# A hybrid recurrent and attention trunk on one core: sums of the readout moved from GpSimd to VectorE, one-input steps moved to ScalarE, and one masked copy of the gated recurrence made a plain copy

## The chip, the cores and the metric

The kernel runs on one core of one Trainium2 chip. The metric is device time in microseconds (us), the median of three runs. A core has five engines that the profile names PE (TensorE matmul; PEld is its weight load), DVE (VectorE), ACT (ScalarE), POOL (GpSimd) and SP (SyncE, which only issues DMAs here). Each engine works through its own queue in order.

## What is computed

Two layers of a trunk over 2048 latent tokens and 256 context tokens, 1024 channels, all in float32. Each layer normalises, projects the channels once, and splits the result into three groups: an RWKV-7 recurrence (6 heads), a gated recurrence (HGRN2, 4 heads) and a windowed attention (6 heads). A readout joins them. Cut to what the change touches:

```python
# gated recurrence, per chunk (b = cumulative sum of log forget gates)
att = jnp.sum(q_c[..., :, None, :] * k_c[..., None, :, :] * jnp.exp(diff), axis=-1)   # lower triangle
out = o_inter + jnp.einsum('zbhts,zbhsv->zbhtv', att, v_c)

# readout of the RWKV heads
yc = y - jnp.mean(y, axis=-1, keepdims=True)
yn = yc * lax.rsqrt(jnp.mean(yc * yc, axis=-1, keepdims=True) + GN_EPS)
yn = yn.reshape(B, T, RWKV_W) * gn_w + gn_b
bonus = jnp.sum(_heads(r) * _heads(k) * r_k, axis=-1, keepdims=True) * _heads(v)
ya = (yn + bonus) * jax.nn.silu(g)
# readout of the gated recurrence
yb = (o * lax.rsqrt(jnp.mean(o * o, axis=-1, keepdims=True) + NORM_EPS)).reshape(...) * norm_w * jax.nn.silu(g)

y = jnp.concatenate([ya, yb, yt], axis=-1) @ w_out[l]
x = x + gate * y
```

## The kernel before

Each layer has three stages. The **input projection** makes all features and writes them to DRAM. The **recurrence stage** (`phase2`) runs four streams side by side: 36 RWKV steps, two directions of the gated recurrence (`Hgrn.window`, nine windows of 256 tokens each), and the attention. The **readout stage** (`Readout`) follows for nine windows of 256 tokens in layer 0 and eight in layer 1, where the context's window is not needed.

The order on each engine is set by a scheduler that replays the program against its own model of durations; `phase2` only hands it the streams in an interleaved order, the readout's at a lower priority. The queues are then fixed: an instruction that waits on the chip holds all that stand behind it on its engine.

`Hgrn.window` builds the attention matrix of a 128-token chunk in levels: a diagonal, then block sizes 1 to 64 (`products`, L1075 to L1085). For each level POOL subtracts (tile `hE`), ACT takes the exponential, DVE multiplies (`hE`, `hQz`), PE multiplies matrices into the PSUM tile `wps` (two buffers, shared with the attention), and the result is copied into `hatt`. At block size 64 the copy is a plain one on ACT. At all others two copies of 64 partitions are made by DVE under a mask (`copy_predicated`, L1085): 14 of them for a window and a direction, of which the block size 32 has two.

`Readout.__init__` splits the output weights, in eight pieces, into a rounded part on ACT (`wohi`) and the remainder on POOL (`wolo`, L1403); this falls into the end of the recurrence stage. `outputs(w)` prepares a window: it adds the two directions (L1455 on DVE, L1456 on POOL), and takes means by matmuls with a constant block matrix. For that `blocks` (L1424) splits its operand into a rounded copy `obh` (a DVE cast, L1430) and a remainder `obl` (DVE), and lets PE multiply both into `ops`. It is called seven times for a window, four times with 512 columns and three with 256. The scales `rk`, `gnw` and the bias `gnb` ride on fused DVE instructions of 256 columns (L83, a helper: `or` is r times k, `oY` the normalised output). At its end ACT rounds the whole result to `ohi`, and the remainder `olo` is made on POOL for the attention's 768 columns and on DVE for the other 1280. `project(w)` then runs 96 matmuls of 512 columns for a window, 24 into each PSUM tile `opo`; DVE multiplies a finished one by the gate (`og`), and POOL adds it to the residual `ox` (L1512). Program order puts `project(w)` beside `outputs` of the next window.

Helper lines: L64 is ACT's activation, L67 a matmul, L74 a two-input operation on DVE or POOL, L83 the fused DVE operation.

Of the kernel before, what the change touches and what calls it, by code (L numbers as in the profile page):

```python
# [9 lines left out]
F32 = mybir.dt.float32  # L10
# [9 lines left out]
L = 2  # L20
# [966 lines left out]
class Hgrn:  # L987
# [23 lines left out]
    def window(self, z, s):  # L1011
# [62 lines left out]

        def products(lhs, rhs, lv, out):  # L1075
            ps = P_([128, 4, 2, 32])
            for u in range(4):
                for e in range(2):
                    t.mm(ps[half[e], u], lhs[:, u, half[e]], rhs(u, e))
            for e in range(2):  # L1080
                o = out(half[e], slice(64 * e, 64 * e + 64))
                m, d = self.lm[half[e], z:z + 1, lv].to_broadcast([64, 8, 32]), ps[half[e]].rearrange("p u x t -> p (u x) t")
                if len(o.shape) == 4:
                    m, d = (a.rearrange("p u (m h) -> p u m h", h=o.shape[3]) for a in (m, d))
                nc.vector.copy_predicated(o, m, d)  # L1085
# [12 lines left out]
        for lv, h in enumerate((64, 32, 16, 8, 4, 2)):  # L1098
# [18 lines left out]
            else:  # L1117
                products(u4(E), lambda u, e: Qz[:, :, u, 32 * e:32 * e + 32], lv - 1, lambda r, c: qh(att[r, :, c]))
            yield
# [268 lines left out]
class Readout:  # L1388


    def __init__(self, t, l, ph):
# [7 lines left out]
        for k in range(KD):  # L1399
            w = ow.tile([128, D], F32, name="wo", tag="wo")  # L1400
            nc.sync.dma_start(out=w, in_=io["w_out"][l, :, k])
            t.act(self.whi[:, k], w, AF.Identity)
            t.tt(self.wlo[:, k], w, self.whi[:, k].bitcast(F32), ALU.subtract, nc.gpsimd)  # L1403
        self.bones = st.tile([128, 128], F32R, name="bonesr")
# [16 lines left out]
    def outputs(self, w):  # L1421
# [3 lines left out]
        def blocks(m, a, n):  # L1425
# [3 lines left out]
            e = cut(self.T_([128, 2, 256], "obl", CFG["bl"], F32R)[:, 0:n])  # L1429
            nc.vector.tensor_copy(h, a)  # L1430
            t.tt(e, a, h.bitcast(F32), ALU.subtract)
# [17 lines left out]
        t.tt(y0, y0, y1, ALU.add, nc.gpsimd if CFG["b2"] else None)  # L1449
        t.tt(Y[:, 3:5], h0, h1, ALU.add, nc.gpsimd)  # L1450
        yv = y0.rearrange("p c (i t) -> p i c t", i=3)
        for i0, n in ((0, 2), (2, 1)):
            ps = blocks(self.cen, yv[:, i0:i0 + n], n)
            t.act(SQ[:, i0:i0 + n], ps[:, 0:n], AF.Square)
            t.act(Y[:, i0:i0 + n], ps[:, 0:n], AF.Identity)  # L1455
        t.act(SQ[:, 3:5], Y[:, 3:5], AF.Square)  # L1456
        for i in range(3):
            t.stt(r[:, i], r[:, i], W(t.P(l, "rk"), i), k[:, i], ALU.mult, ALU.mult)
        yield
# [7 lines left out]
        for i0, n in ((0, 2), (2, 1)):  # L1467
            ps = blocks(self.bones, r[:, i0:i0 + n], n)
            t.tt(v[:, i0:i0 + n], v[:, i0:i0 + n], ps[:, 0:n], ALU.mult)
        hs = load(it(S["sgh"]), "or", [128, 2, 256])  # L1470
        yield
        for i in range(5):
            t.stt(Y[:, i], Y[:, i], W(t.P(l, "gnw"), i) if i < 3 else W(t.P(l, "hnw"), i - 3), SQ[:, i], ALU.mult, ALU.mult)
            if i < 3:
                t.stt(Y[:, i], Y[:, i], W(t.P(l, "gnb"), i), v[:, i], ALU.add, ALU.add)
        t.tt(Y[:, 0:3], Y[:, 0:3], sg, ALU.mult)
# [3 lines left out]
        for a, b, y in ((5, 8, yav), (0, 5, nt(Y))):  # L1480
            t.act(nt(hi[:, a:b]), y, AF.Identity)
            t.tt(nt(lo[:, a:b]), y, nt(hi[:, a:b]).bitcast(F32), ALU.subtract, nc.gpsimd if a == 5 or CFG["b3"] else None)
        self.y[w] = hi, lo
        yield

    def project(self, w, src, dst):
# [8 lines left out]
        for m in range(2):  # L1495
# [3 lines left out]
            for e in range(2):  # L1499
# [10 lines left out]
                else:  # L1510
                    t.tt(o, ps, g[:, d], ALU.mult)
                t.tt(x[:, d], x[:, d], o, ALU.add, nc.gpsimd if l < L - CFG["xa"] else None)  # L1512
                yield
# [137 lines left out]
```

## Time and profile before

| what | value |
|---|---|
| median of 3 runs | 4400.89 us (4397.25 to 4402.82) |
| the profiled execution: its own time, its span | 4410.3 us, 4408.5 us |
| mean granted clock of TensorE | 0.940 |
| PE busy | 3907.5 us (89%), 39424 matmuls |
| DVE busy | 2993.5 us (68%) |
| ACT busy | 2173.6 us (49%) |
| POOL busy | 893.3 us (20%) |

The busy times are sums over the whole span; a busy PE is not a PE at its peak, since matmuls overlap. In time the span is: input projection of layer 0 to about 1120 us, its recurrence stage to about 2000 us, its readout to 2262 us, then the same three for layer 1 to about 3350 us, 4165 us and the end.

### The profile page before, as it was taken

What the parts mean: (1) busy time and instruction counts of PE and PEld (TensorE: products, weight loads), DVE (VectorE), ACT (ScalarE), POOL (GpSimd) and SP (SyncE); (2) the same over time, 40 slices, a digit from 0 to 9 for tenths busy, and PEclk for the clock granted to TensorE, in tenths of its full rate; (3) what the DMA queues carried; (4) which work ended last, traced back from release to release, by engine and by line L of the source; (5) the groups of instructions that cost most, each with busy time, mean ns of one, the idle gap of its engine ahead of it and who ended that gap; (6) DMA issues with size and microseconds to landing.
All of it is one profiled execution on the core that took longest, in us unless ns stands there. A gap on an engine that the chain in (4) does not pass through costs nothing. (4 is left out here: it accounts for less than half of the span.)

```text
span 4408.5 us, 98655 instructions
## 1 busy us (share of the span) xinstructions
PE 3907.5 (89%) x39424; PEld 3188.1 (72%) x39424; DVE 2993.5 (68%) x5698; ACT 2173.6 (49%) x4308; POOL 893.3 (20%) x1038
## 2 busy tenths in 40 slices
PE   7999989999688888967889989989898888998798
PEld 4868867778577777766768877767776777777677
DVE  3426876677577776787853666645775777777787
ACT  3624465654355555543435463455544555555444
POOL 2000011000233322242330000020001323333323
PEclk9999999999799999988989999889998999999899
DMA  5565755676633333346634566445766433334554
GB/s 192 151 203 187 231 166 159 198 223 176 183 108 99 107 111 98 96 113 218 212 125 130 159 212 207 125 120 180 216 201 173 130 93 106 104 98 128 171 178 158
DMA packets 777313, 688.42 MB, mean 156 GB/s; under 512 B 352164, under 2 KB 675044, under 8 KB 776856
## 3 DMA queue, kind: packets, MB, share of 16 engines
q1 hardware_dynamic: 747624, 583.93, 44.4%
q0 software_dynamic: 18720, 68.17, 5.4%
q10 hardware_dynamic: 10512, 30.02, 2.1%
q8 instruction: 312, 5.11, 0.5%
q14 instruction: 145, 1.19, 0.1%
HBM read 440.70 MB, written 241.22 MB: 155 GB/s over the span
## 5 line engine op out<-in xcount | busy, mean ns | idle before, releaser
L67 PE MATMUL ps<-h,whi 128*128 128x512 f32 x4160 | 1372.3, 405 | 27.3 <-ACT s L64 16.6
L67 PEld LDWEIGHTS ps<-h,whi 128*128 128x128 f32 x4160 | 802.3, 194 | 217.9 <-ACT s L64 18.7
L67 PE MATMUL ps<-h,wlo 128*128 128x512 f32 x2080 | 844.4, 406 | 1.6 <-DVE wlo L74 1.6
L67 PEld LDWEIGHTS ps<-h,wlo 128*128 128x128 f32 x2080 | 407.2, 196 | 93.9 <-issue 8.2
L304 POOL DMA_DIRECT2D wraw<-in_w_in_dram x128 | 69.2, 540 | 1669.9 <-DVE wlo L74 1382.3
L74 POOL TENSOR_TENSOR hE<-hb 128x256 f32<-128x256 f32 x408 | 291.3, 736 | 327.9 <-PE wps L67 195.8
L83 DVE SCALAR_TENSOR_TENSOR s<-pb,par,s 128x1024 f32<-128x1024 f32 (+1 forms) x156 | 164.3, 1054 | 182.8 <-ACT s L64 128.4
L1085 DVE COPY_PREDICATED hatt<-lm,wps 64x256 f32<-64x256 int32 x476 | 266.9, 561 | 27.5 <-PE wps L67 21.2
L67 PE MATMUL pq<-KZ,BKs 128*64 128x128 f32 x2496 | 222.8, 292 | 41.5 <-DMA KZ<-scr_RK 25.8
L64 ACT ACT_TABLE_LOAD x171 | 219.4, 1283 | 65.1 <-DVE s L79 20.7
L74 DVE TENSOR_TENSOR hQz<-hE,hqz 128x512 f32<-128x512 f32 x204 | 185.8, 911 | 89.9 <-DMA hqz<-scr_hq 86.8
L67 PE MATMUL opo<-wohi,ohi 128*128 128x512 f32 x544 | 215.7, 413 | 25.4 <-DVE og L74 19.4
L74 DVE TENSOR_TENSOR wlo<-wraw,whi 128x1024 fp32r<-128x1024 f32 x130 | 158.4, 1218 | 95.9 <-ACT whi L64 95.8
L64 ACT ACTIVATE pt<-wps 128x512 f32<-128x512 f32 (+1 forms) x288 | 148.7, 524 | 141.4 <-PE wps L71 138.8
L64 ACT ACTIVATE s<-ps 128x512 f32<-128x512 f32 (+1 forms) x175 | 96.1, 561 | 242.4 <-PE ps L67 211.0
L67 PE MATMUL opo<-wolo,ohi 128*128 128x512 f32 x544 | 212.7, 408 | 0.0
L71 PE MATMUL wps<-ident,prob 128*128 128x128 f32 x960 | 168.9, 293 | 46.0 <-DVE hatt L1085 27.6
L67 PEld LDWEIGHTS pq<-KZ,BKs 128*64 128x64 f32 x2496 | 166.3, 145 | 59.3 <-issue 23.8
L67 PE MATMUL wps<-hQz,hE 128*64 128x64 f32 (+1 forms) x2992 | 149.8, 239 | 56.2 <-DVE hatt L1085 30.8
L74 DVE TENSOR_TENSOR Gs<-can,inv 128x30 f32<-128x30 f32 (+9 forms) x540 | 182.7, 338 | 18.5 <-PE apm L67 7.5
L64 ACT ACTIVATE pb<-ps 128x512 f32<-128x512 f32 (+2 forms) x162 | 79.8, 493 | 233.3 <-PE ps L67 192.4
L64 ACT ACTIVATE hE<-hE 128x512 f32<-128x512 f32 x204 | 128.4, 631 | 131.1 <-POOL hE L74 121.6
(272 smaller groups left out, 9100.7 us busy)
## 6 DMA issues: line engine op xcount, KB each, us to landing
wraw<-in_w_in_dram POOLq DMA_DIRECT2D x128, 512.0 KB, 4.7
scr_KB<-tk SPq DMA_DIRECT2D x36, 768.0 KB
BKs<-scr_KB SPq DMA_DIRECT2D x144, 192.0 KB
KZ<-scr_RK SPq DMA_DIRECT2D x272, 96.0 KB
x<-in_mod_w_dram SPq DMA_DIRECT2D x32, 512.0 KB
lkk<-scr_kk SPq DMA_DIRECT2D x36, 384.0 KB
th<-scr_wa SPq DMA_DIRECT2D x36, 384.0 KB
scr_RK<-lkk SPq DMA_DIRECT2D x36, 384.0 KB
```

The lines of the kernel that those rows point to most:

```text
L64: return self.nc.scalar.activation(out=out, in_=in_, func=func, **kw)
L67: return self.nc.tensor.matmul(out=out, lhsT=lhsT, rhs=rhs, start=start, stop=stop)
L71: return self.nc.tensor.transpose(out, in_, self.ident[0:p, 0:p])
L74: return (eng or self.nc.vector).tensor_tensor(out=out, in0=a, in1=b, op=op)
L83: return (eng or self.nc.vector).scalar_tensor_tensor(out=out, in0=a, scalar=s, in1=b, op0=op0, op1=op1)
L304: (nc.sync, nc.scalar, nc.gpsimd)[CFG["wq"]].dma_start(out=w, in_=io["vw1"][l - 1] if j == 32 else io["w_in"][l, j])
L1085: nc.vector.copy_predicated(o, m, d)
```

## The change

Five things move; what is computed stays the same up to rounding.

- At block size 32 the mask is not needed, because the wanted entries are exactly one quadrant: 32 of the 64 partitions. Two plain copies on ACT of 32 partitions take the place of the two masked DVE copies.
- POOL's four sums in the readout go to DVE: `wolo`, `oY` (the gated recurrence's two directions), `olo` of the attention's columns, and the residual `ox`.
- The rounded copy `obh` in `blocks` goes from DVE to ACT.
- The scales `rk` and `gnw` and the bias `gnb` go to ACT, three instructions of 256 columns each; `gnw` rides on the copy out of PSUM that ACT made anyway.
- What was left of the fused DVE instructions then has no scalar of its own and becomes one two-input instruction of 768 columns each.

```diff
-        def products(lhs, rhs, lv, out):
+        def products(lhs, rhs, lv, out, whole=False):
...
             for e in range(2):
+                if whole:
+                    r = slice(64 * e + 32 * z, 64 * e + 32 * z + 32)
+                    o = out(r, slice(64 * e, 64 * e + 64))
+                    t.act(o, ps[r].rearrange("p u x (m h) -> p (u x) m h", h=32), AF.Identity)
+                    continue
...
-                products(u4(E), lambda u, e: Qz[:, :, u, 32 * e:32 * e + 32], lv - 1, lambda r, c: qh(att[r, :, c]))
+                products(u4(E), lambda u, e: Qz[:, :, u, 32 * e:32 * e + 32], lv - 1, lambda r, c: qh(att[r, :, c]), h == 32)
...
-            t.tt(self.wlo[:, k], w, self.whi[:, k].bitcast(F32), ALU.subtract, nc.gpsimd)
+            t.tt(self.wlo[:, k], w, self.whi[:, k].bitcast(F32), ALU.subtract)
...
-            nc.vector.tensor_copy(h, a)
+            t.act(h, a, AF.Identity)
...
-        t.tt(Y[:, 3:5], h0, h1, ALU.add, nc.gpsimd)
+        t.tt(Y[:, 3:5], h0, h1, ALU.add)
...
-            t.act(Y[:, i0:i0 + n], ps[:, 0:n], AF.Identity)
+            for i in range(n):
+                t.act(Y[:, i0 + i], ps[:, i], AF.Identity, scale=W(t.P(l, "gnw"), i0 + i))
...
-            t.stt(r[:, i], r[:, i], W(t.P(l, "rk"), i), k[:, i], ALU.mult, ALU.mult)
+            t.act(r[:, i], r[:, i], AF.Identity, scale=W(t.P(l, "rk"), i))
+        t.tt(r, r, k, ALU.mult)
...
+            for i in range(i0, i0 + n):
+                t.act(v[:, i], v[:, i], AF.Identity, bias=W(t.P(l, "gnb"), i))
...
-        for i in range(5):
-            t.stt(Y[:, i], Y[:, i], W(t.P(l, "gnw"), i) if i < 3 else W(t.P(l, "hnw"), i - 3), SQ[:, i], ALU.mult, ALU.mult)
-            if i < 3:
-                t.stt(Y[:, i], Y[:, i], W(t.P(l, "gnb"), i), v[:, i], ALU.add, ALU.add)
+        t.tt(Y[:, 0:3], Y[:, 0:3], SQ[:, 0:3], ALU.mult)
+        t.tt(Y[:, 0:3], Y[:, 0:3], v, ALU.add)
+        for i in range(3, 5):
+            t.stt(Y[:, i], Y[:, i], W(t.P(l, "hnw"), i - 3), SQ[:, i], ALU.mult, ALU.mult)
...
-            t.tt(nt(lo[:, a:b]), y, nt(hi[:, a:b]).bitcast(F32), ALU.subtract, nc.gpsimd if a == 5 or CFG["b3"] else None)
+            t.tt(nt(lo[:, a:b]), y, nt(hi[:, a:b]).bitcast(F32), ALU.subtract)
...
-                t.tt(x[:, d], x[:, d], o, ALU.add, nc.gpsimd if l < L - CFG["xa"] else None)
+                t.tt(x[:, d], x[:, d], o, ALU.add)
```

Counted over the program, DVE goes from 5668 instructions to 5497, ACT from 4014 to 4326 (its table loads from 171 to 177) and POOL from 1043 to 925; PE's 26681 matmuls and SP's DMAs stay. The two parts of layer 0 ahead of its recurrence stage are unchanged; from there on the scheduler's order differs on every engine. Three places show how.

DVE in the first window of the gated recurrence of layer 0 (`mx`, `nmx`, `asg` are the attention's, `LK`, `AM` the RWKV recurrence's), before:

```order
L74 TENSOR_TENSOR hE_11125<-hE_11125,hk_10396 128x16x16
L1085 COPY_PREDICATED hatt_10143<-lm,wps 64x8x32 x2
L74 TENSOR_TENSOR mx<-mx 128x2
L74 TENSOR_TENSOR hQz_10153<-hE_11125,hqz_10149 128x512
L83 SCALAR_TENSOR_TENSOR nmx<-mx,nsink 128x2
L74 TENSOR_TENSOR hE_11142<-hE_11142,hk_10251 128x32x8
L74 TENSOR_TENSOR hQz_10152<-hE_11142,hqz_10147 128x512
```

and now:

```order
L74 TENSOR_TENSOR hE_11125<-hE_11125,hk_10396 128x16x16
L74 TENSOR_TENSOR hQz_10153<-hE_11125,hqz_10149 128x512
L74 TENSOR_TENSOR mx<-mx 128x2
L83 SCALAR_TENSOR_TENSOR nmx<-mx,nsink 128x2
L74 TENSOR_TENSOR hE_11142<-hE_11142,hk_10251 128x32x8
L74 TENSOR_TENSOR hQz_10152<-hE_11142,hqz_10147 128x512
```

The masked pair of block size 32 is gone from the queue, and the multiplication `hQz` of a later level follows at once. On ACT the copies now stand behind an exponential of the other direction and an evacuation of the RWKV recurrence:

```order
L64 ACTIVATE ys<-pq 128x384
L64 ACTIVATE hE_11125<-hE_11125 128x512
L64 ACTIVATE hatt_10143<-wps 32x8x32 x2
L64 ACTIVATE pt<-wps 128x256 x2
L64 ACTIVATE hE_11142<-hE_11142 128x512
```

DVE in the readout of layer 0, from the end of one window's outputs into the next, before:

```order
L74 TENSOR_TENSOR oY<-oY,ok 128x768
L1430 CAST obh<-oSQ 128x512
L74 TENSOR_TENSOR og<-opo,gate 128x512 x2
L74 TENSOR_TENSOR obl<-oSQ,obh 128x512
L74 TENSOR_TENSOR olo<-oY,ohi 128x1280
L1430 CAST obh<-oSQ 128x256
L74 TENSOR_TENSOR og<-opo,gate 128x512
L83 SCALAR_TENSOR_TENSOR or<-or,par_91,ok 128x256 x3
```

and now:

```order
L74 TENSOR_TENSOR oY<-oY,ok 128x768
L74 TENSOR_TENSOR og<-opo,gate 128x512
L74 TENSOR_TENSOR obl<-oSQ,obh 128x512
L74 TENSOR_TENSOR ox<-ox,og 128x512 x2
L74 TENSOR_TENSOR olo<-oy_22500,ohi 128x768
L74 TENSOR_TENSOR og<-opo,gate 128x512
L74 TENSOR_TENSOR olo<-oY,ohi 128x1280
L74 TENSOR_TENSOR or<-or,ok 128x768
```

The casts are gone, and the residual sums `ox` and the remainder `olo` of the attention's columns stand between the gate products `og` that free PE's output tiles.

POOL in the last windows of the same readout, before:

```order
L74 TENSOR_TENSOR oY<-oy_23716,oy_23718 128x512
L74 TENSOR_TENSOR olo<-oy_23870,ohi 128x768
L74 TENSOR_TENSOR ox<-ox,og 128x512 x10
L643 MEMSET inv 128x1024
L644 MEMSET can 128x1024
L646 MEMSET XT 128x1536
L74 TENSOR_TENSOR ox<-ox,og 128x512
L374 MEMSET pb 128x2
```

and now, from the last subtraction of the recurrence stage on:

```order
L74 TENSOR_TENSOR hE_21893<-hb_21162 128x128x2 x2
L304 DMA wraw<-in_w_in_dram 128x1024
L643 MEMSET inv 128x1024
L644 MEMSET can 128x1024
L646 MEMSET XT 128x1536
L374 MEMSET pb 128x2
```

POOL has nothing left to do between the recurrence stage and the clears for layer 1.

## Rows read from the trace of the kernel before

**Rows 1.** Windows: stretch, us; busy PE PEld DVE ACT POOL (count); clock, DMA, GB/s
```profile
1150.00:1870.00 720.00, 624.00 (x10210) 522.57 (x10211) 527.34 (x1040) 379.40 (x1056) 223.86 (x261) 0.95 0.41 110
...
1870.00:2002.00 132.00, 84.64 (x1588) 74.03 (x1589) 98.18 (x157) 52.55 (x108) 55.82 (x55) 0.83 0.49 143
4040.00:4165.00 125.00, 90.13 (x1643) 80.34 (x1639) 91.42 (x146) 50.22 (x106) 47.27 (x43) 0.84 0.54 151
2002.00:2262.00 260.00, 236.41 (x1064) 193.07 (x1063) 194.99 (x315) 95.25 (x126) 82.31 (x56) 0.95 0.56 185
4165.00:4409.00 244.00, 217.15 (x1140) 176.47 (x1140) 189.22 (x302) 111.17 (x162) 75.64 (x47) 0.95 0.54 177
```
**Rows 2.** Waits of PE, layer 1's readout: waiter, releaser, us in total, times, longest
```profile
PE opo L67 <- DVE og L74: 8.6, 7, 2.4
```
**Rows 3.** Timeline, layer 0's readout: start, us, engine, operation, count
```profile
2117.17 0.39 PE L67 MATMUL opo<-wohi,olo 128*128 128x512 f32 x1
...
2118.55 2.23 PE L67 MATMUL opo<-wohi,olo 128*128 128x512 f32 x9
```
**Rows 4.** Timeline of DVE, layer 1's readout: first and last window's last step
```profile
4181.11 1.48 DVE L74 TENSOR_TENSOR olo<-oY,ohi 128x1280 fp32r<-128x1280 f32 x1
...
4379.49 2.04 DVE L74 TENSOR_TENSOR olo<-oY,ohi 128x1280 fp32r<-128x1280 f32 x1
```
**Rows 5.** Tile hatt: copies (ns min/median/max), and who waited for them
```profile
L1085 DVE COPY_PREDICATED hatt<-lm,wps x476: 391/449/758, 1208.3 to 4128.0; 64x256 f32<-64x256 int32 x159
L64 ACT ACTIVATE hatt<-wps x68: 360/379/386, 1222.8 to 4092.7; 64x256 f32<-64x256 f32 x68
...
  PE wps L67: 47.9, 55
...
  PE wps L71: 27.6, 30
```
**Rows 6.** Groups by shape, POOL and DVE: count, busy us, mean ns, idle before
```profile
L74 POOL TENSOR_TENSOR wolo<-wo,wohi 128x1024 fp32r<-128x1024 f32 x16 | 39.0, 2438 | 38.5 <-ACT wohi L64 33.1 <-PE pq L71 5.1
...
L74 DVE TENSOR_TENSOR wlo<-wraw,whi 128x1024 fp32r<-128x1024 f32 x130 | 158.4, 1218 | 95.9 <-ACT whi L64 95.8
```
**Rows 7.** Timelines of POOL and DVE, end of layer 0's recurrence stage
```profile
1959.58 2.54 POOL L74 TENSOR_TENSOR wolo<-wo,wohi 128x1024 fp32r<-128x1024 f32 x1
...
1959.82 2.84 DVE L74 TENSOR_TENSOR hQz<-hE,hqz 128x512 f32<-128x512 f32 x1
```
**Rows 8.** Tiles hQz, or, oY: DVE's ns min/median/max
```profile
L74 DVE TENSOR_TENSOR hQz<-hE,hqz x204: 673/686/2843, 1122.3 to 4120.8; 128x512 f32<-128x512 f32 x102
...
L83 DVE SCALAR_TENSOR_TENSOR or<-or,par,ok x51: 471/479/2065, 1993.7 to 4361.2; 128x256 f32<-128x256 f32 x51
L1430 DVE CAST obh<-or x34: 281/418/1550, 2000.5 to 4368.3; 128x512 fp32r<-128x512 f32 x17, 128x256 fp32r<-128x256 f32 x17
...
L74 DVE TENSOR_TENSOR oY<-oY,ok x17: 933/949/959, 2012.1 to 4377.2; 128x768 f32<-128x768 f32 x17
...
L74 DVE TENSOR_TENSOR olo<-oY,ohi x17: 1477/1493/3135, 2014.4 to 4379.5; 128x1280 fp32r<-128x1280 f32 x17
```
**Rows 9.** Groups by shape, DVE in both readouts
```profile
L83 DVE SCALAR_TENSOR_TENSOR or<-or,par,ok 128x256 f32<-128x256 f32 x51 | 36.9, 773 | 12.8 <-DMA ok<-scr_k 11.1 <-DMA or<-scr_r 1.7
...
L74 DVE TENSOR_TENSOR olo<-oY,ohi 128x1280 fp32r<-128x1280 f32 x17 | 32.2, 1893 | 6.9 <-ACT ohi L64 6.7
...
L1430 DVE CAST obh<-or 128x512 fp32r<-128x512 f32 x17 | 13.7, 803 | 0.0
```
**Rows 10.** Groups by shape, ACT: nearest prices for what it takes over
```profile
L64 ACT ACTIVATE h<-hf 128x512 fp32r<-128x512 f32 x64 | 39.1, 624 | 103.3 <-DVE hf L80 70.7 <-PE opo L67 25.5 <-PE pa L71 6.7
...
L64 ACT ACTIVATE t<-s,par 128x256 f32<-128x256 f32 x6 | 3.0, 505 | 6.7 <-DVE s L83 6.7
```
**Rows 11.** Groups by shape, POOL in both readouts
```profile
L74 POOL TENSOR_TENSOR ox<-ox,og 128x512 f32<-128x512 f32 x68 | 98.8, 1464 | 245.4 <-DVE og L74 225.2 <-DVE oY L83 7.3 <-issue 6.0
...
L74 POOL TENSOR_TENSOR olo<-oy,ohi 128x768 fp32r<-128x768 f32 x17 | 36.2, 2130 | 60.2 <-ACT ohi L64 32.6 <-DMA ov<-scr_v 18.3 <-issue 5.9
```

## The prediction

> **What bounds the kernel now.** I read the profile in this order: busy time by stretch, then PE's waits in each stretch, then the groups of instructions by shape, then timelines where a group's mean and median lie apart. In the windows by stretch [rows 1] the reader is to see that PE is the busiest engine everywhere, and that the stretches differ in how much of it stands idle: 96 of 720 us in the recurrence of layer 0, 47 of 132 us and 35 of 125 us at the ends of the two recurrence stages, 24 of 260 us and 27 of 244 us in the readouts, of which the last 9 us lie behind PE's last matmul. DVE comes second, at 73 to 78%. ACT is at 53% in the recurrence and 37 to 46% in the readouts. So a DVE instruction saved is worth only what PE waits for it, and ACT has room.
>
> In the readout of layer 1 PE's largest wait is for DVE's gate product [rows 2]. Matmuls of 512 columns follow each other every (2.23 - 0.39) / 8 = 0.23 us [rows 3]; 0.39 us is the length of a single one beside them. A window has 96 of those and 22 of half the width in `ops`, so PE needs 96 x 0.23 + 22 x 0.115 = 24.6 us for it. It takes (4379.49 - 4181.11) / 7 = 28.3 us [rows 4]. DVE is busy 77% of that stretch, about 22 us a window. The 3.7 us between 28.3 and 24.6 is what the change could win there, for each window, and no more.
>
> **Part 1, the plain copies in the recurrence.** 68 masked copies leave DVE. At their median of 0.449 us that is 31 us; ACT gets 68 copies at 0.379 us, 26 us (the row has 64 partitions, the new ones 32; I take it unchanged) [rows 5]. PE waited for the masked copies 47.9 + 27.6 = 75.5 us in all [rows 5]. Two of the 14 copies of a window move, so their share is 10.8 us. ACT is less loaded than DVE (53 against 73%) and its copy shorter, but now it stands behind an exponential. I take **-8 us**, with the other DVE work moving up included. Bounds: -18, if everything that queues on DVE gains too; +10, if PE waits as long again for ACT.
>
> **Part 2, the output weights' remainder.** 16 instructions on POOL took 39.0 us, and POOL stood idle another 38.5 us before them, with the subtractions of the gated recurrence behind them [rows 6]. On DVE the same shape costs 1.218 us, 19.5 us in all [rows 6]. But POOL's were not free for DVE: beside one of 2.54 us DVE's `hQz` took 2.84 us [rows 7], against a median of 0.686 [rows 8]. If each of the 16 held DVE by 2.15 us, DVE gets 34 us back for the 19.5 it takes on. These fall into the ends of the recurrence stages, where PE idles 82 us in sum and the gated recurrence is last. I guess that half of the 16 stand in its chain: 8 x (2.44 - 1.22) gives **-10 us**. Bounds: -22 (all 16, and DVE's stalls too); +10 (DVE, at 73 to 74% there, is late by half of what it takes on).
>
> **Part 3, the readout.** For a window DVE loses seven casts (four of 0.418 us, three of 0.281), three `or` of 0.479 and six `oY` of about the same, 6.8 us. It gains four instructions of 768 columns at 0.949 us and five of 512 columns, which by the slope between 768 and 1280 columns (0.949 and 1.493 us) cost 0.68: 7.2 us [rows 8]. By these medians the change adds 0.4 us to DVE. The means lie above the medians: `or` by 51 x (0.773 - 0.479) = 15.0 us, `olo` by 17 x 0.40 = 6.8, the cast of `or` by 17 x 0.385 = 6.5 [rows 8, 9]. That is 28 us for three groups, 1.7 us a window; I read it as DVE held by POOL, as in [rows 7], and take 2.0 with the smaller groups. POOL works on nothing in the readout afterwards, so DVE's net gain is 2.0 - 0.4 = 1.6 us a window, 24 us for the 15 windows that follow each other. PE, which mostly waits for DVE there, gets three quarters of it: -18 us.
>
> The Trainium skill says of such pairs (SBUF — State Buffer, "Who interferes with whom") that VectorE and GpSimd share one pair of ports, that an instruction holds it for its whole length, and that the other engine then stands still. The trace's 2.84 beside 2.54 us agrees with it. By the full rule every POOL instruction there could cost DVE its own length; what the sum would be is the first rival below.
>
> ACT takes on, for a window, four casts of 0.624 us, and three casts and six scaled steps of 256 columns, each at 0.505 at most [rows 10]: 7.0 us, and somewhat for the copy out of PSUM cut in three. In layer 1 it was busy 111 us for eight windows, 14 us each [rows 1]; it comes to 21 of about 27 us. That hides, except where a window is alone. At the start of a readout nothing covers the chain from loads to `ohi`; there three scales of 0.505 us and casts that are 0.2 us longer than DVE's add about 2 us for each layer: +4. Part 3 is **-14 us**. Bounds: -36 (PE's idle 24 + 18 us all gone, less the start's part) and +33, the third rival.
>
> **Part 4, the ends.** The last residual sum of each layer takes 1.46 us on POOL [rows 11] and 0.68 on DVE: **-1 us**. POOL's own queue gains nothing else: the clears for layer 1 behind `ox` wait for PE's last matmuls anyway. SP's stores of `ox` go out as much earlier; the other DMAs keep their issuers.
>
> **Sum.** -8 - 10 - 14 - 1 = -33 us, made against the profiled execution's own 4410.3 us: 4377. That execution is 9.4 us above the median of 4400.9, so for a median I predict **4368 us**. Everything from layer 0's recurrence on is ordered anew by the scheduler; the bounds hold that too.
>
> **The rivals.**
>
> *The lock takes everything.* If each POOL instruction of the readout cost DVE its length, four `ox` of 1.46 us and one `olo` of 2.13 make 8.0 us a window [rows 11], far above PE's 3.7. The readouts would go at PE's pace: -36 in place of -14, and part 2 would give 5 more. That is 4368 - 22 - 5 = 4341 us. For it speaks the stall in [rows 7]; against it that three groups' excess holds only 1.7 us a window. The page's rule, in the section named above, is the same mechanism.
>
> *Nothing of it is on the path.* PE's waits for DVE are then waits for a chain (matmul, cast, remainder, matmul), which is no shorter with a link on ACT. Part 3 gives +4, part 2 nothing, part 1 -8: 4397 us. For it speaks that the wait in [rows 2] sums to only 8.6 us. Against it, DVE's stalls lie in these very chains.
>
> *DVE takes over POOL's wait.* `olo` of the attention's columns needs `ohi` from ACT, and POOL stood 32.6 us for it [rows 11]. Now DVE stands there, with the gate products behind it that free PE's output tiles, and ACT, with 7 us more to do for a window, delivers later. If all 32.6 us reach PE and part 3 gives no gain, the sum is -8 - 10 - 1 + 33 + 4 = +18: 4419 us, slower. It decides from the point where DVE's waits for `ohi` pass 1.6 us a window, the whole of its gain. Against it: the new order puts another instruction or two ahead of most of these `olo`.
>
> **How the numbers follow.** A measurement of this kernel tells about 0.2%, 9 us, from no change. The forecast has a chance of 0.60, with 4348 to 4392 us as its own range; the lock 0.15; nothing on the path 0.14; DVE's new wait 0.11. Forecast and lock are faster, 0.75; the same 0.14; slower 0.11. The range of 8 in 10 holds the forecast's, most of the lock's and the case without effect: 4335 to 4402 us.
>
> **What would show it.** Right: in the readouts no DVE group's mean lies over its median by more than a few per cent; layer 1's windows follow every 26 to 27.5 us; PE idles under 15 us in each readout; at the ends of the recurrence stages `hQz` has no instruction above 1.5 us while `wolo` runs, and the stretches are some 5 us shorter each. Wrong: PE waits for ACT's `obh` or `hatt` by over 10 us in sum; DVE waits for ACT's `ohi` by 25 us; or the recurrence stages differ by more than 20 us either way, which would make the scheduler's new order, and not the moved work, the cause.

## The result, and the profile after

The changed kernel takes 4426.44 us (median of four runs, 4415.59 to 4430.49), against 4399.91 us of the kernel before in the same comparison: a ratio of 1.0057 with a 95% interval of 1.0042 to 1.0073. It is slower by 0.57%, 26 us. The forecast was 4368 us and faster, the range reached to 4402: both missed. The profiled execution took 4430.49 us with a span of 4428.6 us.

In what follows a readout's length is the time from the start of its first `opo` matmul to the start of its last. The windows by stretch, cut at just these two times, show the two readouts of the changed kernel:

```profile
core 0: us, PE busy (x) PEld busy (x) DVE busy (x) ACT busy (x) POOL busy (x), PEclk, DMA share, GB/s
2004.40:2267.30 262.90, 234.18 (x1058) 190.42 (x1058) 165.68 (x255) 144.53 (x242) 1.35 (x2) 0.96 0.55 181
4160.60:4420.00 259.40, 224.45 (x1097) 180.96 (x1096) 163.46 (x246) 157.17 (x264) 0.00 (x0) 0.91 0.46 155
```

and the same two stretches of the kernel before:

```profile
2003.00:2259.30 256.30, 235.05 (x1060) 192.07 (x1058) 192.86 (x312) 94.61 (x126) 78.61 (x54) 0.95 0.56 186
4171.00:4399.30 228.30, 211.51 (x1089) 172.31 (x1090) 183.02 (x291) 105.21 (x154) 74.39 (x46) 0.97 0.54 178
```

Layer 0's readout grew by 6.6 us and layer 1's by 31.1 us; all other stages together shrank by 17.6 us, which makes the 20.1 us between the two spans. (Layer 0's readout starts 1.4 us later than before, 18.4 us less lie between the two readouts, and 0.6 us less behind the second.) The reader is to see that DVE and POOL were unloaded and yet both readouts took longer. DVE is busy 46.7 us less in the two readouts, POOL does next to nothing, ACT has 101.9 us more and stands at 55% and 61%. No engine but PE is near full, and PE idles more: 28.7 and 34.9 us, against 21.2 and 16.8 before. The window's period in layer 1, 28.3 us before [rows 4], is (4400.7 - 4172.3) / 7 = 32.6 us, by the first and the last `olo` of that readout:

```profile
L74 DVE TENSOR_TENSOR olo<-oY,ohi x8: 1483/1488/1493, 4172.3 to 4400.7; 128x1280 fp32r<-128x1280 f32 x8
```

DVE's relief came as forecast, and more: the lines of tiles `or` and `olo` on DVE have no spread left (minimum, median and maximum in ns), where the longest `or` of 256 columns was 2.07 us and the longest `olo` 3.14 us before [rows 8].

```profile
L74 DVE TENSOR_TENSOR or<-or,ok x17: 948/957/960, 1995.4 to 4370.7; 128x768 f32<-128x768 f32 x17
```

```profile
L74 DVE TENSOR_TENSOR olo<-oY,ohi x17: 1481/1486/1493, 2017.2 to 4400.7; 128x1280 fp32r<-128x1280 f32 x17
```

The waits of layer 1's readout say who holds whom now. Each line is waiter, releaser, us in total, times, and the longest. Changed kernel:

```profile
ACT obh L64 <- PE ops L67: 34.2, 9, 5.6
DVE obl L74 <- ACT obh L64: 21.6, 13, 6.4
PE opo L67 <- ACT ohi L64: 17.7, 6, 5.2
PE opo L67 <- DVE og L74: 9.5, 6, 2.1
```

Kernel before:

```profile
ACT oSQ L64 <- PE ops L67: 46.6, 17, 5.3
...
PE opo L67 <- DVE og L74: 8.6, 7, 2.4
...
PE opo L67 <- ACT ohi L64: 3.3, 3, 1.9
```

PE's wait for DVE's gate product [rows 2] is about what it was. New is PE's wait for ACT's `ohi`, the rounded result with which a window's 96 matmuls begin: 17.7 us in place of 3.3. In layer 0 this wait grew as much, from 2.7 to 17.9 us, but there PE's waits for DVE fell, for `og` from 10.8 to 8.4 us and for `obl` from 3.8 us to nothing, so that PE idles only 7.5 us more. ACT's timeline of one such window shows why `ohi` is late (start, us, operation, and in brackets how long ACT stood idle before it and for whom):

```profile
4246.32 0.63 ACT L64 ACTIVATE obh<-oSQ 128x512 fp32r<-128x512 f32 x1 [5.59 <-PE ops L67]
4246.97 1.28 ACT L64 ACT_TABLE_LOAD   x1
4248.27 0.69 ACT L64 ACTIVATE oSQ<-ops,epsg 128x512 f32<-128x512 f32 x1
...
4252.73 1.28 ACT L64 ACT_TABLE_LOAD   x1
4254.03 0.29 ACT L64 ACTIVATE ofs<-ofs,eps 128x1 f32<-128x1 f32 x1
...
4255.17 1.28 ACT L64 ACT_TABLE_LOAD   x1
4256.46 0.69 ACT L64 ACTIVATE oSQ<-ops,eps 128x512 f32<-128x512 f32 x1
...
4257.96 1.28 ACT L64 ACT_TABLE_LOAD   x1
4259.26 1.27 ACT L64 ACTIVATE oSQ<-oSQ 128x1280 f32<-128x1280 f32 x1
...
4266.56 0.91 ACT L64 ACTIVATE or<-or,par 128x256 f32<-128x256 f32 x2 [1.30 <-DMA or<-scr_r]
4267.38 0.40 ACT L64 ACTIVATE obh<-oSQ 128x256 fp32r<-128x256 f32 x1
4267.68 0.49 ACT L64 ACTIVATE or<-or,par 128x256 f32<-128x256 f32 x1
...
4269.85 1.25 ACT L64 ACTIVATE ohi<-oY 128x1280 fp32r<-128x1280 f32 x1
```

Three things stand ahead of `ohi`. A cast waits 5.59 us for PE's `ops` matmuls, which have to release one of the two buffers of `obh`. The logarithm behind it (`epsg`) reads what matmuls of the same group write, so this row alone does not show that the cast made it late: before the change ACT's steps that read `ops` stood 46.6 us for PE themselves. The root of layer 1's last normalisation (`ofs`) falls between two logarithms, so that the table is loaded three times in 6.5 us. And the scaled step `or` of the *next* window stands ahead of this window's `ohi` and waits for its DMA. Meanwhile PE has nothing to do from about 4266 to 4271 us.

### The profile page after: what moved, and what is told of

The parts are those of the page before. It is cut to its first block, busy times and chain, and to the rows that moved or that the text cites. A ratio compares the mean times of both kernels' runs of the same rounds, so it can differ in the third digit from the quotient of the medians.

```text
span 4428.6 us, 98611 instructions
## 1 busy us (share of the span) xinstructions
PE 3926.2 (89%) x39424; PEld 3203.4 (72%) x39424; DVE 2918.3 (66%) x5527; ACT 2303.4 (52%) x4620; POOL 706.0 (16%) x920
## 5 line engine op out<-in xcount | busy, mean ns | idle before, releaser
L67 PEld LDWEIGHTS ps<-h,whi 128*128 128x128 f32 x4160 | 797.0, 193 | 220.7 <-issue 18.1
L67 PE MATMUL pq<-KZ,BKs 128*64 128x128 f32 x2496 | 229.1, 298 | 46.7 <-DMA KZ<-scr_RK 26.4
L67 PE MATMUL opo<-wohi,ohi 128*128 128x512 f32 x544 | 221.4, 425 | 53.5 <-ACT ohi L64 35.6
L1091 DVE COPY_PREDICATED hatt<-lm,wps 64x256 f32<-64x256 int32 x408 | 236.6, 580 | 22.3 <-PE wps L67 16.8
L71 PE MATMUL wps<-ident,prob 128*128 128x128 f32 x960 | 170.3, 295 | 47.9 <-DVE hatt L1091 25.8
L74 DVE TENSOR_TENSOR Gs<-can,inv 128x30 f32<-128x30 f32 (+9 forms) x540 | 182.5, 338 | 18.2 <-PE apm L67 7.1
L74 DVE TENSOR_TENSOR inv<-inv,Gs 128x30 f32<-128x30 f32 (+9 forms) x540 | 181.3, 336 | 11.7
```

Source lines behind the costliest of these rows:

```text
L67: return self.nc.tensor.matmul(out=out, lhsT=lhsT, rhs=rhs, start=start, stop=stop)
L71: return self.nc.tensor.transpose(out, in_, self.ident[0:p, 0:p])
L74: return (eng or self.nc.vector).tensor_tensor(out=out, in0=a, in1=b, op=op)
```

## The experiments

Each row below gives a ratio to the kernel before on the same chip, with its interval, and the lengths of the two readouts from one profile. The kernel before took 4411 to 4414 us on the chips of these runs; the expectations name times against the 4400 us of the first comparison, so a measured time is to be held against them by its ratio. Lengths scatter: three kernels with one readout code took 262.9, 268.6 and 267.3 us in layer 0, and two 259.4 and 253.6 us in layer 1, each in another order of the scheduler. Steps of 6 us are read as nothing, so that of the two readouts' growth layer 1's is the one that counts.

| kernel | ratio | readout of layer 0, us | of layer 1, us | PE idle in layer 1 | table loads there |
|---|---|---|---|---|---|
| before | 1 | 256.3 | 228.3 | 16.8 | 22 |
| changed | 1.0057 [1.0042, 1.0073] | 262.9 | 259.4 | 34.9 | 28 |
| casts back on DVE | 1.0015 [1.0000, 1.0030] | 264.4 | 236.2 | 23.5 | 27 |
| scales back on DVE | 1.0009 [0.9994, 1.0023] | 261.6 | 246.3 | 27.6 | 30 |
| both back | 0.9950 [0.9934, 0.9967] | 248.3 | 234.6 | 19.5 | 27 |
| before, casts and scales moved | 1.0078 [1.0052, 1.0104] | 257.8 | 250.8 | 30.1 | 26 |
| before, sums moved | 0.9984 [0.9973, 0.9996] | 250.6 | 233.0 | 21.3 | 24 |
| before, plain copies | 0.9994 [0.9980, 1.0009] | 259.0 | 228.9 | 18.1 | 22 |
| changed, masked copies back | 1.0051 [1.0030, 1.0072] | 267.3 | 253.6 | 32.1 | 27 |
| changed, four obh, no wolo | 0.9987 [0.9971, 1.0002] | 255.5 | 239.7 | 25.9 | 29 |
| changed, two oY and others, no wolo | 0.9969 [0.9953, 0.9985] | 250.9 | 240.7 | 21.4 | 30 |
| changed, no root | 1.0043 [1.0025, 1.0062] | 268.6 | 243.6 | 29.6 | 15 |
| changed, all three | 0.9964 [0.9946, 0.9981] | 251.2 | 216.6 | 9.2 | 15 |
| both back, layer 1's ox on POOL | 0.9941 [0.9921, 0.9961] | 248.5 | 227.2 | 16.0 | 21 |

### Which part costs

The first theory was that the casts cost (they stand in ACT's queue), the second that the scaled steps do (more hops in a window's chain), the third that DVE had taken over POOL's waits.

**Casts back.** The changed kernel with

```diff
-            t.act(h, a, AF.Identity)
+            nc.vector.tensor_copy(h, a)
```

> The changed kernel with the rounded copies obh back on DVE; all else as changed. Theory 1 (a cast on ACT stands in its queue for PE's matmuls and holds the logarithms and exponentials behind it): layer 1's readout, 293 us from the last product of the recurrence to the last output matmul against 263 before, falls to 260 to 272, and the time to 4385 to 4405 us. Theory 2 (the nine scaled steps lengthen the chain of a window): it stays above 280, the time at 4415 to 4428. Theory 3 (DVE inherits POOL's waits with the sums): no change, 4420 to 4430.

**Scales back.** The steps of `rk`, `gnw` and `gnb` as in the kernel before, the rest as changed:

```diff
-            t.act(r[:, i], r[:, i], AF.Identity, scale=W(t.P(l, "rk"), i))
-        t.tt(r, r, k, ALU.mult)
+            t.stt(r[:, i], r[:, i], W(t.P(l, "rk"), i), k[:, i], ALU.mult, ALU.mult)
...
```

> The changed kernel with rk, gnw and gnb back in the fused DVE instructions; casts stay on ACT. Theory 1: little, 4415 to 4428 us, and ACT's waits in obh for PE stay at 30 to 40 us in layer 1's readout. Theory 2: layer 1's readout falls under 272 us and the time to 4385 to 4405. Theory 3: 4420 to 4430.

**Both back.** The two edits above together; what stays of the change is POOL's sums on DVE and the plain copies.

> The changed kernel with casts and scales back on DVE: what is left is the sums from POOL to DVE and the plain copies. Theories 1 and 2 both: 4365 to 4390 us, since DVE then no longer stands for POOL and ACT's chain is as before. Theory 3 (DVE inherits POOL's waits, or is too full: 27 us of work a window against PE's 24.6): 4410 to 4435 us.

Either part undone takes back 0.42% and 0.48%, both together 1.07%, 47 us, and the kernel is then faster than before. Against 4400 us the ratios are 4406, 4404 and 4378 us. Layer 1's stretch as the expectations measure it, from the last product of the recurrence, is 269.8 us with the casts back, inside the first theory's range, and 278.2 us with the scales back, longer than the second theory's 272. The windows of this kernel's readouts:

```profile
2007.30:2255.60 248.30, 231.25 (x1060) 189.33 (x1058) 187.49 (x363) 95.63 (x126) 1.40 (x2) 0.97 0.60 192
4150.70:4385.30 234.60, 215.14 (x1096) 174.17 (x1096) 181.71 (x335) 112.00 (x160) 0.00 (x0) 0.96 0.53 171
```

DVE carries 40 us more than in the changed kernel, and PE idles 27 us less. So the third theory falls: with POOL's sums on DVE this kernel is 0.50% faster than the one before. That gain is not in the readouts, which together are only 1.7 us shorter than before (8.0 us less in layer 0, 6.3 more in layer 1). The first two theories both hold in part, and neither is enough. In layer 1 undoing the casts alone brings 23 of the 25 us that undoing both brings, undoing the scales alone 13; in layer 0 the readout stays long as long as either one is on ACT (264.4 and 261.6 us), and is short only without both (248.3).

**Casts and scales alone.** The kernel before with these two edits, POOL's sums and the masked copies as they were. This asks whether the moves would have paid had DVE still been held by POOL.

```diff
-            nc.vector.tensor_copy(h, a)
+            t.act(h, a, AF.Identity)
...
-            t.stt(r[:, i], r[:, i], W(t.P(l, "rk"), i), k[:, i], ALU.mult, ALU.mult)
+            t.act(r[:, i], r[:, i], AF.Identity, scale=W(t.P(l, "rk"), i))
+        t.tt(r, r, k, ALU.mult)
...
```

> The kernel before with the casts and the scales moved to ACT, and nothing else: POOL keeps its four sums and the masked copies stay. Undone from the changed kernel the two cost 1.1 % together. Theory 1 and 4, ACT in the chain: the cost is the same with POOL's sums in place, for it is not DVE's load that matters: slower than before by 0.5 to 1.2 %, layer 1's readout 250 to 265 us against 228.3. Theory 6, relief where it is needed: with POOL holding DVE in the readout, DVE is the bound, so taking 6.8 us a window off it pays there: 0 to 0.5 % faster than before, layer 1 under 228 us; the loss in the changed kernel then came of moving POOL's sums and the rest at once.

It is slower by 0.78%, layer 1's readout takes 250.8 us, and PE waits 14.0 us there for `ohi`. Layer 0's readout, 257.8 us, is within the scatter of what it was, and 21 us more lie between the readouts (1933.1 us in place of 1911.7), which nothing here explains. Taking work from DVE bought nothing even where POOL still stalls it; in layer 1's readout the loss belongs to the steps on ACT. The sixth theory falls.

### What ACT is late with

Three remedies, each against one of the three things in the timeline. Two need room in SBUF and get it by leaving out `wolo`: its matmuls read `wohi` again, so PE has as many of them, the output gets that product twice and the remainder's term not at all, and DVE makes 16 subtractions fewer. What is read of them is the readouts' length, not the time. A kernel with `wolo` left out and nothing else was not run, so what this alone does to the lengths is not shown.

**Four buffers for the casts.**

```diff
-            h = cut(self.T_([128, 2, 256], "obh", 2, F32R)[:, 0:n])
-            e = cut(self.T_([128, 2, 256], "obl", CFG["bl"], F32R)[:, 0:n])
+            h = cut(self.T_([128, 2, 256], "obh", 4, F32R)[:, 0:n])
+            e = cut(self.T_([128, 2, 256], "obl", 4, F32R)[:, 0:n])
```

> The changed kernel with four buffers in place of two for the rounded copy obh and its remainder obl. To make room the remainder wolo of the output weights is left out: its matmuls read wohi a second time, so PE has as many matmuls, and the 16 DVE subtractions at the ends of the recurrence stages are not made (16 x 1.22 = 20 us of DVE, some of which may leave the time as well; so the readouts are to be read by their own length, from the first opo matmul to the last, 262.9 us in layer 0 and 259.4 us in layer 1 of the changed kernel, 256.3 and 228.3 before). Theory 1, the casts: ACT stands 39 us for PE's ops matmuls because it needs an obh buffer back, and all that is behind the cast in its queue stands too. Then those waits nearly vanish (under 10 us in layer 1), PE's wait for ohi falls from 17.7 us to under 8, and layer 1's readout comes down to 235 to 245 us, near that of the kernel with the casts on DVE (236.2). Theory 4, the serial window: a window has one oY and one oSQ, so the next one can't begin before olo has read oY; each hop on ACT makes that chain longer whatever buffers the casts have. Then layer 1 stays above 250 us. Theory 5, table loads: no change, 259 us.

```profile
4156.40:4396.10 239.70, 213.75 (x1105) 174.11 (x1106) 164.48 (x247) 160.56 (x267) 0.00 (x0) 0.96 0.53 172
```

The length is in the first theory's range; its waits are not. ACT still stands 21.8 us for `ops` (34.2 before it), and PE 12.2 us for `ohi`. Buffers are a part of it.

**Two buffers for a window's tiles.** `oY`, `oSQ`, `or`, `ok` and `ov` get two each.

```diff
-        Y, SQ = self.T_([128, 5, 256], "oY"), self.T_([128, 5, 256], "oSQ")
+        Y, SQ = self.T_([128, 5, 256], "oY", 2), self.T_([128, 5, 256], "oSQ", 2)
...
```

> The changed kernel with two buffers in place of one for oY, oSQ and for the loaded or, ok, ov; to make room the remainder wolo is left out as in the run with four obh, and the readouts are read by their own length. Theory 4, the serial window: the period of 32.6 us in layer 1 is the length of the chain from a window's first sum into oY to olo's last read of it, so with a second oY the windows overlap: layer 1's readout falls to 225 to 238 us, its period to under 29 us, PE's wait for ohi to under 8 us, and layer 0's readout to under 255. Theory 1, the casts: obh has two buffers still and ACT waits 39 us in layer 1 for PE to release them; then layer 1 stays over 248 us and that wait over 25. Theory 5, table loads and ACT's load as such: no change, over 255 us, since ACT has as much to do.

240.7 us lies between what the two theories gave; layer 0, at 250.9, did what the fourth said. PE's wait for `ohi` fell to 6.8 us with no less work on ACT (160.5 us busy), so ACT's load as such is not the limit. ACT's wait for `ops` fell with it, to 15.9 us, which the first theory had above 25. Where the windows may overlap, most of PE's wait for `ohi` is hidden, though the readout is still 12.4 us longer than before.

**No root.** The root of layer 1's last normalisation becomes an identity; the computation lacks it.

```diff
-                t.act(st[:, 1:2], st[:, 0:1], AF.Sqrt, bias=t.eps6, scale=1.0 / D)
+                t.act(st[:, 1:2], st[:, 0:1], AF.Identity, bias=t.eps6, scale=1.0 / D)
```

> The changed kernel with the square root of the last normalisation (layer 1's end, 128 x 1) made an identity on ACT, which leaves the root out of the computation; with it go ACT's table loads for it. In layer 1's readout ACT made 27 table loads of 1.28 us, 22 in the kernel before. Theory 5, table loads: that only layer 1 lost 31 us comes from them: they stand in ACT's queue between the steps of a window's chain. Without the root 14 to 16 remain, ACT gets 14 to 16 us back, nearly all of it in the chain, and layer 1's readout falls from 259.4 to 243 to 248 us; the time falls by 0.25 to 0.4 % against the changed kernel. Theories 1 and 4 alone: the loads lie in ACT's idle time; layer 1's readout stays within 5 us of 259.

ACT's table loads in layer 1's readout, by groups of operations (count, busy us, mean ns, idle before), in the changed kernel and without the root:

```profile
L64 ACT ACT_TABLE_LOAD x28 | 35.9, 1283 | 0.5
```

```profile
L64 ACT ACT_TABLE_LOAD x15 | 19.2, 1283 | 0.3
```

13 loads, 16.7 us, went, and the readout came from 259.4 to 243.6 us, 15.8 us shorter, as the fifth theory said. The two numbers are alike in part by luck: only 5.3 of the 15.8 us are less idle time of PE, 10.5 are less busy time of the same matmuls, at a granted clock of 0.96 in place of 0.91, and from the 253.6 us that the same readout code took in another order it would be 10 us. PE's wait for `ohi` did not fall (19.4 us), nor did ACT's for `ops` (38.4 us). The time fell by only 0.14%, less than expected, and the two intervals overlap; layer 0's readout, whose code is untouched, came out 5.7 us longer in the new order. Only layer 1 has the root, so it is a candidate for why layer 1 lost so much more than layer 0. That is not shown: the kernel before has the root too and was not run without it, and the length does not go with the number of loads, of which 27 stand beside 234.6, 236.2 and 253.6 us.

**All three at once**, the edits above in one kernel, `wolo` and the root left out.

> The changed kernel with all three remedies of the runs before at once: four buffers for obh and obl, two for oY, oSQ, or, ok and ov, and no square root in the last normalisation. The remainder wolo and the root are left out of the computation. If the loss of 31 us in layer 1's readout is the sum of what a window's chain waits for (casts for buffers 20 us, single tiles 19 us, table loads 16 us, each alone), all three give at least the length of before, 228 us, and with PE as the bound 205 to 225 us: 8 windows of 24.6 us by PE's pace are 197 us, and a start and an end. If the three cure the same microseconds, it stays at 236 to 244 us, and ACT's busy time or DMA is what is left. Layer 0: 242 to 252 us.

```profile
4165.40:4382.00 216.60, 207.38 (x1094) 170.84 (x1092) 157.29 (x240) 135.39 (x247) 0.00 (x0) 0.98 0.58 186
```

PE idles 9.2 us, its wait for `ohi` is gone from the list, and ACT waits 2.2 us for `ops`. The three took 19.7, 18.7 and 15.8 us singly, 54 in sum, and 42.8 together: they are different microseconds for the most part. So the moved work fits on ACT, 135 us busy of 217, with PE hardly waiting for it. The readout is 11.7 us shorter than before the change, but the kernel before has the root and `wolo`, and this one has neither; the second buffers with the root in place were not run together. That the loss came of the steps' place in a queue where each window hands over to the next through single tiles is what the three runs point to; how much of the 42.8 us leaving out the root or `wolo` makes is open.

### What the other parts were worth

**Plain copies alone**, on the kernel before (the branch `whole` in `products` as the change has it):

```diff
-                products(u4(E), lambda u, e: Qz[:, :, u, 32 * e:32 * e + 32], lv - 1, lambda r, c: qh(att[r, :, c]))
+                products(u4(E), lambda u, e: Qz[:, :, u, 32 * e:32 * e + 32], lv - 1, lambda r, c: qh(att[r, :, c]), h == 32)
```

> The kernel before with the plain copies at block size 32 alone. As forecast, -8 us (4388 to 4396). If the copies on ACT cost the recurrence: 4405 to 4415, both recurrence stages longer. If only the scheduler's new order shows: within 5 us of before, and the readouts, whose code is unchanged, differ by up to 10 us.

**Sums alone**, POOL's four sums to DVE on the kernel before, of which `oY` is one:

```diff
-        t.tt(Y[:, 3:5], h0, h1, ALU.add, nc.gpsimd)
+        t.tt(Y[:, 3:5], h0, h1, ALU.add)
...
```

> The kernel before with POOL's four sums moved to VectorE and nothing else. With the plain copies these gave a ratio of 0.9950 (with casts and scales undone), the plain copies alone 0.9994. If the sums carry that gain and the copies nothing, the ratio is 0.993 to 0.998. If the copies only pay once the sums are moved, it is 0.998 to 1.002. Layer 0's readout 246 to 252 us against 256.3; layer 1's, where ACT's squares of the last normalisation now wait for DVE's ox, 229 to 236 against 228.3.

**Masked copies back**, on the changed kernel, the edit of the plain copies the other way round:

> The changed kernel with the masked copies of block size 32 back on DVE, all else as changed. The plain copies alone gave a ratio of 0.9994 [0.9980, 1.0009] on the kernel before; but the sums alone gave 0.9984 and the sums with the copies 0.9950, a difference of 0.34 %, 15 us. If the copies are worth 15 us once POOL's sums have gone to DVE, this kernel is slower than the changed one: a ratio of 1.008 to 1.0105 against its 1.0057, and the two recurrence stages longer by 10 to 20 us together. If they are worth what they gave alone, 1.0045 to 1.0075, and the 0.34 % were another order of the whole program.

The sums alone gain 0.16%, less than the 0.2 to 0.7% expected of them if they carried the gain; their readouts (250.6 and 233.0 us) are those of the kernel with both parts back, within the scatter. The copies gain 0.06% alone, and the changed kernel without them is 0.06% faster and not slower (1.0057 to 1.0051), both inside the intervals: nothing that can be told. That leaves 0.3% between the sums alone and the sums with the copies which the copies don't explain by themselves. In the two profiles 11 us of it lie ahead of layer 0's readout, which starts at 2018.4 us with the sums alone and at 2007.3 with both. It may be another order of the whole program; no run settles it.

Where the sums pay can be read from the readouts' starts and ends. Between the two readouts the three kernels that leave all four sums on POOL take 1911.7, 1916.8 and 1933.1 us, the eleven others 1884.4 to 1899.2. Layer 0's readout starts at 1993.6 to 2003.0 us in the three, and at 2001.0 to 2018.4 us in the eleven. So the gain lies between the readouts, and some of it is lost ahead of the first. How much of either is the moved sums and how much the new order, these runs don't separate.

**A version that beats both.** Both parts back on DVE, and the residual sum of layer 1 left on POOL:

```diff
-                t.tt(x[:, d], x[:, d], o, ALU.add)
+                t.tt(x[:, d], x[:, d], o, ALU.add, nc.gpsimd if l == L - 1 else None)
```

> The change without casts and scales, and with the residual sum ox of layer 1 left on POOL (layer 0's goes to DVE): plain copies, wolo, oY and olo on DVE in both layers. With casts and scales undone layer 1's readout was 234.6 us, 6 us longer than before (228.3), with 27 table loads of ACT in place of 22; the order of this kernel has 23. If the ox on DVE is what the 6 us are for, by its place in DVE's queue or by the table loads that it shifts, layer 1 comes to 222 to 230 us, layer 0 stays at 246 to 252 us, and the time is 0.10 to 0.25 % below that of 0.9950: a ratio of 0.992 to 0.995. If POOL's ox holds DVE as the prediction priced it (1.46 us each, 32 of them), layer 1 comes to 234 us or more and the ratio to 0.995 or above.

```profile
2003.00:2251.50 248.50, 233.16 (x1058) 190.21 (x1058) 187.48 (x363) 95.52 (x126) 1.32 (x2) 0.96 0.60 192
4142.50:4369.70 227.20, 211.17 (x1098) 171.72 (x1096) 177.67 (x305) 103.61 (x154) 48.70 (x31) 0.98 0.56 177
```

0.9941 [0.9921, 0.9961], 4386.08 us against 4413.43 on that chip, is the fastest kernel of the study. Layer 1's readout is 7.4 us shorter than with `ox` on DVE, little more than the scatter, with six table loads fewer; which of the two did it was not separated. Against 0.9950 the time itself is not told apart.

## Why the prediction was wrong

**The step that failed** is in part 3: ACT's 7 us more for a window, "That hides, except where a window is alone", with +4 us for the two starts. Part 3 was to bring -14 us, at worst +33; the two readouts grew by 37.7 us. The amount of ACT's work was right: 101.9 us over 17 windows is 6.0 us each, and ACT came to 157 us for eight windows in layer 1, 20 us each, where 21 was forecast. What was wrong was to set a busy time against a period. Undoing the two moves gives 47 us back. ACT's steps are links of a window's chain, from the first sum into `oY` to `ohi`, and the next window must wait for the single `oY` to be read. An in-order engine with 39% idle time still delivers late if the instruction that PE needs stands behind one that waits for PE, for a table or for a DMA.

**The gain of part 3** is the other half. DVE's relief was to be 1.6 us net for a window; 46.7 us of busy time over 17 windows is 2.7 us, more than said, and the means of `or` and `olo` are their medians. That POOL held DVE is shown by layer 1's `olo` in three kernels, before, with `ox` alone left on POOL (the last kernel of the experiments), and with all four sums moved but the rest as before:

```profile
L74 DVE TENSOR_TENSOR olo<-oY,ohi x8: 1483/2206/3135, 4181.1 to 4379.5; 128x1280 fp32r<-128x1280 f32 x8
```

```profile
L74 DVE TENSOR_TENSOR olo<-oY,ohi x8: 1479/1492/2039, 4149.3 to 4349.8; 128x1280 fp32r<-128x1280 f32 x8
```

```profile
L74 DVE TENSOR_TENSOR olo<-oY,ohi x8: 1476/1492/1494, 4173.3 to 4377.8; 128x1280 fp32r<-128x1280 f32 x8
```

With casts and scales moved and POOL's sums left, the longest of both layers is still 2.42 us. The Trainium skill's rule of the shared ports (SBUF — State Buffer, "Who interferes with whom"), by which one of the two engines holds the pair and the other stands still, agrees with these rows. But "PE gets three quarters of it" was a guess without a row: with casts and scales on DVE, POOL's sums moved gave layer 0's readout 8.0 us and layer 1's nothing (+6.3 us). The wait of 8.6 us for `og` [rows 2] stayed at 9.5. The case for the rival "nothing of it is on the path" was this row, and for layer 1 it was the better reading; in layer 0 PE's waits for DVE did fall, by 6.2 us.

**Part 1**, -8 us: the mechanism holds and the time doesn't show it. PE's waits for `hatt` fell from 75.5 us [rows 5] to 37.0 + 25.8 = 62.8 us, close to the 10.8 less of the forecast; with the copies alone they are 60.2 us, with the masked copies back 75.1. Yet the copies move the total by 0.06%, within the measurement. **Part 2**, -10 us: `hQz` had nothing above 1.22 us at the ends of the recurrence stages, as forecast, against 2.84 before [rows 7]. Its own price was not run alone; all sums together, readout included, are worth 0.16%, 7 us. Of the 18 us of parts 1 and 2 layer 0 shows nothing, since its readout starts 1.4 us later; the 18.4 us between the readouts hold a new order too. **Part 4** was right by its sign: the step from the last `opo` matmul to the end went from 9.2 to 8.6 us.

**The rivals.** "DVE takes over POOL's wait" had the side right and the cause wrong: DVE's `olo` waited 13.8 us for `ohi` in both readouts, not 25, and the sums by themselves are a gain. "The lock takes everything" did not come: DVE got 2.7 us a window back and not 8.0, and the readouts did not go at PE's pace even with casts and scales on DVE. The slower case was there to be priced in the text ("ACT delivers later"), but only as the condition of DVE's wait, and not as PE's own. Of the signs set out, PE's wait for ACT by more than 10 us is the one that came, by way of `ohi`: 35.6 us in the two readouts. PE's wait for `obh` is above 10 us as well, 17.8 us, but it lies ahead of the two readouts, and PE waited 18.2 us in sum for DVE's cast before, so that sign tells nothing.

## What to carry to other kernels

Before a step is moved to an engine with room, read that engine's queue, not its share: which instruction does the busiest engine wait for, and what will now stand ahead of it, waiting for what? Where windows hand over through single tiles, add the step to the chain's length and not to the engine's load; test it by giving the chain a second tile. Where a root, a logarithm and an exponential share one in-order engine, count the table loads anew after a step is moved: here they went from 21 to 30 in one stage, from kernel to kernel, with the root in all of them. And two parts of a change that cost are best undone one by one and together: here either one alone kept layer 0 slow.

## What the hardware showed

A wait of PE can cost more than its length. The timeline of PE in the changed kernel's window of above, and its windows with the granted clock (the number after the five busy times):

```profile
4265.80 0.63 PE L67 MATMUL opo<-wolo,ohi 128*128 128x512 f32 x1
4271.16 0.79 PE L67 MATMUL opo<-wohi,ohi 128*128 128x512 f32 x1 [4.73 <-ACT ohi L64]
...
4272.18 0.63 PE L67 MATMUL opo<-wohi,ohi 128*128 128x512 f32 x1
4272.60 0.63 PE L67 MATMUL opo<-wolo,ohi 128*128 128x512 f32 x1
...
4276.32 0.39 PE L67 MATMUL opo<-wohi,ohi 128*128 128x512 f32 x1
4276.55 0.39 PE L67 MATMUL opo<-wolo,ohi 128*128 128x512 f32 x1
```

```profile
4262.00:4266.00 4.00, 2.11 (x8) 1.47 (x8) 3.93 (x8) 2.01 (x4) 0.00 (x0) 0.92 0.42 139
4266.00:4271.00 5.00, 0.43 (x2) 0.00 (x0) 2.75 (x4) 4.43 (x8) 0.00 (x0) 0.50 0.65 207
...
4273.00:4276.00 3.00, 3.00 (x9) 2.34 (x8) 2.39 (x5) 1.33 (x4) 0.00 (x0) 0.56 0.59 184
4276.00:4280.00 4.00, 4.00 (x21) 3.33 (x20) 1.04 (x1) 0.51 (x1) 0.00 (x0) 1.00 0.80 229
```

PE ran haltingly and then stood for 4.73 us; the granted clock went to 0.50, the lower of its two levels, 1.2 of 2.4 GHz. When `ohi` came, the matmuls followed each other every 0.43 us in place of 0.23 [rows 3] for some ten matmuls, 2 us more. Over layer 1's readout the granted clock fell from 0.97 to 0.91, and PE was busy 224.45 us for the matmuls that took 211.51 before. Of the 31.1 us that this readout lost, 12.9 are this longer busy time and 18.1 the waits themselves. The prediction had priced a wait at its length. The surcharge is not in proportion to the waits: in this readout PE idles 29.6 us at a clock of 0.96 without the root, and 21.4 us at 0.94 with two buffers for a window's tiles.
